# Storing the output projection's rows to DRAM, two more weight buffers, and a new order of the last loads

## The chip, the cores and the metric

The kernel runs on one core of a Trainium2 chip. The metric is the device time of one execution in microseconds. Before the change it is 557.77 us, the median of three runs (557.16 to 558.68).

The engines are named as in the profile: PE is TensorE's matmul and PEld its weight load, DVE is VectorE, ACT is ScalarE, POOL is GpSimd, SP is SyncE, which here only issues transfers. Each has its own queue of instructions, worked off in order.

## The reference

One layer of a decoder trunk on 512 rows of 1024 float32 numbers. Its first part (three kinds of mixers sharing one input and one output projection) ends in `h = h + mix @ w_out`. Then follow the two parts that the change touches:

```python
h = h + hier_moe(rmsnorm(h, norm2_g), router_group_w, ..., exp_w_gate, exp_w_up, exp_w_down)
gate = sigmoid(rmsnorm(h, ple_norm_g) @ ple_gate_w + ple_gate_b)
e = p @ ple_proj_w
h = h + gate * e
return rmsnorm(h, final_norm_g)
```

`hier_moe` picks for every row one group of experts and two experts in it, of 32 in all. Each expert is a gated MLP with two 1024x256 matrices (gate, up) and one 256x1024 matrix (down): 3 MB of weights each, 96 MB together.

## The kernel before, in words

The 512 rows are four tiles of 128 (NT = 4). `h1` holds the rows after the output projection, one tile of 128x1024 each, and stays in SBUF to the end.

**Experts.** They are worked in 16 pairs. A pair gathers up to 64 rows for each of its two experts, from a copy of the normed rows in DRAM (`tnd`), turns them (`xt`), and computes `gu` (gate and up, 16 products), `hid` and `dn` (down, 16 products). The result goes back by an indirect DMA to a table `yd` in DRAM that has two rows for each row of the input. The first pair takes its rows from `h1` by products with a 0/1 matrix (`spread`, L974). The last pair's result is not sent through DRAM: it is added to h1 by products with a 0/1 matrix (`scatter`, L1051), after its rounding error has been split off so that two fast products give full precision.

**Weights.** An expert's weights are three units of 1 MB. A unit takes a buffer from the front of a list, `ring`; a buffer returns to it when the products that read it are recorded, and the transfer itself waits until they have run. `load_units` records loads as long as the ring has buffers. A load also waits until the third load before it has landed (AHEAD = 3). All these transfers, and those of the last stage, are issued by SP in the order in which they are written; that order is fixed by hand, as is PE's order, and ACT's and DVE's from pair 14 on.

**The last stage.** After pair 14, SP loads what the end needs: `load_y(t)`, the two returned rows per input row for tile t (1 MB); the four quarters of the gate matrix (`gate_load`, 1 MB each); and two vectors copied to all partitions (`rows`, 0.5 MB each). The gate product is done in three fast products per block, so the matrix is split: `gate_hi(k, hf)` on ACT scales and rounds block k of column half hf, `gate_lo` on DVE takes the remainder (L1075). For a tile, `add_y` adds the returned rows to h1 (two adds of 128x1024), `scatter` adds the last pair's rows, `turn` transposes the sum and splits it (L1221 to L1224), `rms` takes its mean square (with a power on POOL, L63), `last` runs 48 products per tile (`pg`, L1242), and `finish` does the rest on DVE and ACT (L1252 to L1262) and stores the output. `at` in `tail` puts other work between the products: `prep(t + 1)` turns the next tile, `sums(t)` adds the rows of a later one. Between the last pair's products and the first gate product PE runs 24 products of `pe` (p @ ple_proj_w), which are otherwise spread over the pairs by the table PLE.

Of the kernel before, what the change touches and what calls it, by code (L numbers as in the profile page):

```python
# [27 lines left out]

FILL = (8, 3, 0, 1, 0, 1, 0, 1, 0, 1, 1, 1, 4, 2, 2, 2, 9)

PLE = (5, 1, 1, 1, 1, 1, 1, 1, 1, 1, 1, 1, 1, 1, 2)
PLE_LAST = (4, 4, 4)
AHEAD = 3
NR, NL = 4, 9
CLEAR = (7, 8, 9, 10)
# [53 lines left out]
def mixers(ctx, tc, A, K, dbg):  # L89
# [360 lines left out]
    sbctx.close()  # L450
    pctx.close()
    hp = ctx.enter_context(tc.tile_pool(name="hp", bufs=1, side="left"))
    h1 = K["h1"] = [hp.tile([P, D], F32, name=f"h1_{t}") for t in range(NT)]
    for t in range(NT):
        nc.sync.dma_start(h1[t], A["x"][t * P:(t + 1) * P, :])
    parts = (step for t in range(NT) for hf in range(2) for step in out_proj(nc, K, mixh, mixl, hf, t, WO_EARLY))
# [157 lines left out]
def ffn(ctx, tc, A, K, mixh, mixl, out, dbg, stage):  # L614
# [67 lines left out]

    slab, loads = {}, []

    def load_units(m=96):

        while ring and m and len(slab) < 96:
            n, m = len(slab), m - 1
            n = n - n % 6 + (0, 3, 1, 4, 2, 5)[n % 6]
            slab[n] = unit(F32, [P, 2048])  # L690
            loads.append(nc.sync.dma_start(slab[n], A["w_exp"][n // 3, n % 3]).ins)
            if len(loads) > AHEAD:
                tc.add_manual_dep(loads[-1], loads[-1 - AHEAD].name,
                                  mybir.DependencyInfo(mybir.DependencyClass.Sync, mybir.DependencyReason.DATA))
# [20 lines left out]
    def ple_steps():  # L715

        pT, pW = pl_in
        for j in range(8):
            t, hf = j // 2, j % 2
            p = ps("pe", "sc" if j < 5 else "gu")  # L720
            for c in range(2):
                for k in range(2):
                    n = hf * 512 + c * 256
                    PE.matmul(p[:, c * 256:c * 256 + 256], pT[:, k * S + t * P:k * S + (t + 1) * P], pW[:, k, n:n + 256],  # L724
                              start=(k == 0), stop=(k == 1))
                    if c == k == 1:
                        kept.append((t, hf, p))
                        ple_out()
                    yield
# [14 lines left out]
    V.tensor_copy(cm.rearrange("p a b -> p (a b)"), cmf)  # L744
    V.tensor_tensor(rw, rw, g2c[:, :, None].to_broadcast([P, KC, 36]), ALU.mult)
    tnd = dram.tile([S, D], F32, name="tnd")
    Ab = mw.tile([P, NT, 32], BF, name="Ab")
    pr_ = cw.tile([P, 448], F32, name="pr", tag="cmf")
    posA = pr_[:, :128].rearrange("p (t e) -> p t e", t=NT)
# [87 lines left out]
    def weights(t, g8, e8, id2, c0):  # L837
# [21 lines left out]
        V.tensor_tensor(pe(c0), pe(cw), rt(0), ALU.subtract)  # L859
        V.tensor_copy(rt(1), pe(c0))  # L860
        V.tensor_tensor(rt(2), pe(c0), rt(1), ALU.subtract)

    chosen = {}
    halves = [(t, hf) for t in range(NT) for hf in range(2)]
# [181 lines left out]
    def scatter(j):  # L1046

        t, hf = j // 2, j % 2
        sc = ps("sc", "sc")
        for q in range(2):  # L1050
            PE.matmul(sc, DTs[15][:, t], out_[15][hf][q], start=(q == 0), stop=(q == 1))  # L1051
        y = h1[t][:, 512 * hf:512 * hf + 512]
        V.tensor_tensor(y, y, sc, ALU.add)


    gr, gw = [], {}
# [20 lines left out]
            free(gr[2 * hf + k // 4])  # L1077

    order.enter_context(tc.manual_schedule(engines={mybir.EngineType.PE}))
    load_units(1)  # L1080
    with tc.manual_schedule(engines={mybir.EngineType.DVE}):
        run(steps[0])
        for t in (0, 1):
# [15 lines left out]
        for hf in range(2):  # L1099
            gather_T(0, hf)  # L1100
        one_hot(1, NT - 1)
    ple_load()
    load_units()

# [56 lines left out]
    def add_y(t, rs=(0, 1)):  # L1161

        for r in rs:
            V.tensor_tensor(h1[t], h1[t], ys[t][:, r], ALU.add)  # L1164

    def load_y(t):
        ys.append(unit(F32, [P, 2, D]))
        nc.sync.dma_start(ys[t], yd.rearrange("(r n) d -> n r d", r=2)[t * P:(t + 1) * P])

    ends = ExitStack()  # L1170
    for i in range(16):
# [16 lines left out]
        free(slab[6 * i + 2], slab[6 * i + 5])  # L1188
        load_units()
        if i == 14:  # L1190
            load_y(0)
            for j in range(4):
                gate_load(j)
            load_y(1)
            rows = mix.tile([P, 2, D], F32, name="rows", tag="m0")
            nc.sync.dma_start(rows[:, 0], bcast(A["ple_gate_b"]))
            load_y(2)
            nc.sync.dma_start(rows[:, 1], bcast(A["final_norm_g"]))
            load_y(3)


# [72 lines left out]
    def tail(sums=None):  # L1274

        for t in range(NT):
            at = {}
            if t + 1 < NT:
                at[1, 1] = lambda: prep(t + 1)
            if sums and t == 0:  # L1280
                at[0, 6] = lambda: sums(1)
            if sums and t + 2 < NT:
                at[1, 5] = lambda: sums(t + 2)
            last(t, at)

    def sums(t):
        add_y(t)
        for hf in range(2):
            scatter(2 * t + hf)

    down(15, lambda n: n < 2 and add_y(0, (n,)))
    ple(PLE_LAST[0])
    gate_hi(0, 0)
    for hf in range(2):
        scatter(hf)
    gate_lo(0, 0)
    gate_hi(1, 0)
    ple(PLE_LAST[1])
    lo = [turn(0, hf) for hf in range(2)]
    ple(PLE_LAST[2])  # L1300
    free(pl_in[1])
    for f in lo:
        f()
    gate_lo(1, 0)
    for k in range(2, KC):
        gate_hi(k, 0)
        gate_lo(k, 0)
    count_beyond()
    for k in range(KC):
        gate_hi(k, 1)  # L1310
        gate_lo(k, 1)
    ov_slots = ring[:3]
    junk, h3s = (unit(F32, shape, slot) for shape, slot in zip(([P, 2, 512], [P, 4, 512]), ring[3:]))
    SC.preload_act_table_set("sigmoid_and_others")
    rms(0)
    tail(sums)
    ends.close()
# [157 lines left out]
```

## Time and profile before

| | us |
|---|---|
| median of 3 runs | 557.77 |
| the profiled execution | 556.99 |
| its span | 555.2 |
| PE busy | 514.5 (93% of the span) |
| DVE busy | 276.2 (50%) |
| ACT busy | 210.8 (38%) |
| POOL busy | 87.1 (16%) |
| DMA moved | 148.82 MB, 268 GB/s over the span |

The share of busy time is a mean over stages with different limits. In the timeline a row gives the start, the busy time, the engine, the line, the operation, output and inputs, and in square brackets the idle time of the engine just before it with what ended that. In the chain of waits a row gives start, duration and what the end of the program waited for there. SPq stands for SP's queue of transfers.

### The profile page before, as it was taken

How to read it: one execution, taken by the hardware profiler on the slowest of the kernel's cores; microseconds unless marked ns; L12 is line 12 of the kernel's file. 1: busy time of each engine (PE TensorE's matmuls, PEld its weight loads, DVE VectorE, ACT ScalarE, POOL GpSimd, SP SyncE). 2: the span in 40 equal slices, each digit the busy share in tenths (PEclk: the TensorE clock that was granted, in tenths of full speed). 3: DMA queues.
4: the chain of work that ended last, by engine and by line, in shares of the span. 5: the costliest groups of instructions: out<-in, count | busy, mean ns of one | idle time of the engine just before them, and what ended most of it. 6: DMA issues, size and time to landing. Idle time of an engine off the chain costs nothing.

```text
span 555.2 us, 7581 instructions
## 1 busy us (share of the span) xinstructions
PE 514.5 (93%) x2713; PEld 325.3 (59%) x2713; DVE 276.2 (50%) x735; ACT 210.8 (38%) x443; POOL 87.1 (16%) x122
## 2 busy tenths in 40 slices
PE   8899999999999999999999999998798987949992
PEld 5797886876997788844333333332233332638872
DVE  6762957756747565773422322221121111597764
ACT  7466665646766434411112111110111101473352
POOL 3301111221008500002111111111110000011110
PEclk9999999999999999999999999999999999988997
DMA  8882222300339669989999999999999999950111
GB/s 303 265 325 73 62 72 71 91 26 2 117 126 418 251 263 413 348 337 387 416 412 417 399 394 387 375 383 396 368 399 418 416 418 390 416 211 0 40 44 73
DMA packets 35641, 148.82 MB, mean 268 GB/s; under 512 B 6557, under 2 KB 14109, under 8 KB 22160
## 3 DMA queue, kind: packets, MB, share of 16 engines
q1 hardware_dynamic: 29984, 137.46, 64.3%
q0 software_dynamic: 4320, 7.95, 3.8%
q10 hardware_dynamic: 1296, 2.89, 1.3%
q8 instruction: 23, 0.38, 0.3%
q14 instruction: 18, 0.15, 0.1%
HBM read 139.61 MB, written 16.25 MB: 281 GB/s over the span
## 4 chain that ended last, share of the span: by engine, by line
PE 62%; DMA 18%; DVE 9%; ACT 7%; issue 2%; POOL 1%; SPq 0%; ACTq 0%; DVEq 0%; POOLq 0%
DMA unit<-in_w_exp_dram 17%; PE gu L997 12%; PE pj L234 9%; PE po L80 8%; PE dn L1029 7%; PE pj L257 5%; PE z L257 4%; PE z L311 2%; PE po L333 2%; PE pe L724 2%; ACT unit L1071 2%; PE x L974 1%; DVE h L1164 1%; PE pl L780 1%; PE z L292 1%
## 5 line engine op out<-in xcount | busy, mean ns | idle before, releaser
L997 PE MATMUL gu<-unit,xT 128*64 128x512 f32 x512 | 127.5, 598 | 13.1 <-DMA unit<-in_w_exp_dram 13.1
L997 PEld LDWEIGHTS gu<-unit,xT 128*64 128x64 f32 x512 | 37.0, 137 | 85.0 <-issue 59.2
L1029 PE MATMUL dn<-unit,hidT 128*64 128x512 f32 x256 | 60.6, 599 | 1.7 <-ACT hidT L1020 0.8
L234 PE MATMUL pj<-xh,wp 128*128 128x512 f32 x176 | 51.2, 398 | 0.4 <-ACT wp L69 0.4
L1242 PE MATMUL pg<-unit 128*128 128x512 f32 (+1 forms) x216 | 47.9, 378 | 0.8 <-ACT unit L735 0.6
L1002 ACT ACTIVATE sg<-gu 128x256 f32<-128x256 f32 x16 | 6.1, 383 | 110.5 <-PE gu L997 110.5
L1003 DVE SCALAR_TENSOR_TENSOR hid<-sg,wsl,gu 128x256 f32<-128x256 f32 x16 | 7.7, 478 | 79.6 <-ACT sg L1002 79.5
L1242 PEld LDWEIGHTS pg<-unit 128*128 128x128 f32 x216 | 37.9, 193 | 9.0 <-ACT unit L735 0.7
L1043 POOL DMA_INDIRECT yd<-big,idy x15 | 15.1, 1009 | 163.8 <-ACT big L1033 163.8
L1029 PEld LDWEIGHTS dn<-unit,hidT 128*64 128x64 f32 x256 | 19.7, 137 | 32.0 <-issue 24.2
L234 PEld LDWEIGHTS pj<-xh,wp 128*128 128x128 f32 x176 | 32.6, 188 | 8.2 <-ACT wp L69 1.3
L1033 ACT ACTIVATE big<-dn 128x512 f32<-128x512 f32 x30 | 17.9, 597 | 50.0 <-PE dn L1029 50.0
L930 DVE COPY SL<-sl 128x10 f32<-128x10 f32 (+1 forms) x17 | 2.8, 167 | 66.0 <-PE sl L929 66.0
L70 DVE TENSOR_TENSOR wp<-wraw,wp 128x768 fp32r<-128x768 f32 (+2 forms) x28 | 25.8, 927 | 13.6 <-ACT wp L69 13.4
L69 ACT ACTIVATE wp<-wraw 128x768 fp32r<-128x768 f32 (+2 forms) x28 | 22.8, 817 | 20.2 <-PE pj L234 9.8
L234 PE MATMUL pj<-xl,wp 128*128 128x512 f32 x88 | 29.4, 401 | 0.0
L986 DVE TENSOR_TENSOR xT<-xt,g2c 128x512 f32<-128x512 f32 x30 | 20.6, 687 | 11.8 <-PE xt L985 11.7
L80 PE MATMUL po<-wo,mx 128*128 128x512 f32 x96 | 25.7, 408 | 0.0
L257 PE MATMUL pj<-wp,xh 128*128 128x384 f32 x96 | 24.8, 351 | 0.0
L80 PE MATMUL po<-unit,mx 128*128 128x512 f32 x96 | 24.1, 399 | 0.0
L943 POOL DMA_INDIRECT xg<-tnd,idx x15 | 15.4, 1029 | 33.7 <-issue 16.0
L985 PEld LDWEIGHTS xt<-ident,xg 128*128 128x128 f32 x120 | 13.4, 141 | 11.5 <-issue 11.4
(293 smaller groups left out, 881.2 us busy)
## 6 DMA issues: line engine op xcount, KB each, us to landing
unit<-in_w_exp_dram SPq DMA_DIRECT2D x96, 1024.0 KB, 8.7
wraw<-in_w_in_dram SPq DMA_DIRECT2D x20, 384.0 KB, 3.5
yd<-zero SPq DMA_DIRECT2D x4, 1024.0 KB, 7.9
unit<-yd SPq DMA_DIRECT2D x4, 1024.0 KB, 6.5
unit<-in_ple_gate_w_dram SPq DMA_DIRECT2D x4, 1024.0 KB
wraw<-in_w_out_dram SPq DMA_DIRECT2D x8, 256.0 KB, 3.0
h<-in_x_dram SPq DMA_DIRECT2D x4, 512.0 KB
unit<-in_w_out_dram SPq DMA_DIRECT2D x4, 512.0 KB, 7.8
```

The source lines that it names most:

```text
L69: nc.scalar.activation(h, src, AF.Copy)
L70: nc.vector.tensor_tensor(l, src, h.bitcast(F32), ALU.subtract)
L80: nc.tensor.matmul(p, a[k][:, ts_], K["wo"][k][:, b, hs], start=(n == 0), stop=(n == 3 * len(ks) - 1))
L234: PE.matmul(q, a[:, i * P:(i + 1) * P], b[k], start=(n == 0), stop=(n == 3 * KC - 1))
L257: PE.matmul(p[t][:, :W_IN[j]], a[k][:, t * P:(t + 1) * P], b, start=(n == 0), stop=(n == 3 * KC - 1))
L943: G.indirect_dma_start(out=xg[i % 2], out_offset=None, in_=tnd, in_offset=bass.IndirectOffsetOnAxis(ap=idx[:, i:i + 1], axis=0), bounds_ch ...
L986: V.tensor_tensor(xTs[i, hf], p.rearrange("p (a b) -> p a b", a=4), g2c[:, 4 * hf:4 * hf + 4, None].to_broadcast([P, 4, P]), ALU.mult)
L997: PE.matmul(gu[64 * e:64 * e + 64], xTs[i, k // 4][:, k % 4, 64 * e:64 * e + 64], w[e][k // 4][:, 512 * (k % 4):512 * (k % 4) + 512], star ...
L1029: PE.matmul(dn[64 * e:64 * e + 64], hT[:, f, 64 * e:64 * e + 64], w[e][2][:, 1024 * f + 512 * hf:1024 * f + 512 * hf + 512], start=(f == 0 ...
L1033: SC.activation(o[:, 512 * hf:512 * hf + 512], dn, AF.Copy)
L1043: G.indirect_dma_start(out=yd, out_offset=bass.IndirectOffsetOnAxis(ap=idy[:, i:i + 1], axis=0), in_=o, in_offset=None, bounds_check=2 * S ...
L1242: PE.matmul(p, hT[t][:, a, ks], gw[k][:, b, hs], start=start and n == 0, stop=stop and n == len(ab) - 1)
```

## The change

h1 becomes two buffers of two tiles each. As soon as all four tiles are complete they are stored to a DRAM tensor `hd`, and when the first pair has read them, the two buffers join the ring as two more units. Two more weight loads are recorded ahead of these stores. Near the end h1 is loaded back: tile 0 ahead of the last two weight units, the others between the returned rows. The first gate quarter is loaded ahead of tile 0's returned rows and partly split inside the last pair's down step. The adds of the returned rows move from DVE to POOL for tiles 1 to 3. The last pair's rows are added to tile 1 behind the weight splits, by products recorded earlier. More `pe` products go into the pairs, so that 4 are left for the end.

```diff
-PLE = (5, 1, 1, 1, 1, 1, 1, 1, 1, 1, 1, 1, 1, 1, 2)
-PLE_LAST = (4, 4, 4)
+PLE = (5, 1, 1, 1, 1, 1, 2, 2, 2, 2, 2, 2, 2, 2, 2)
+PLE_LAST = 4
...
-    h1 = K["h1"] = [hp.tile([P, D], F32, name=f"h1_{t}") for t in range(NT)]
+    K["hp"] = hp
+    hh = [hp.tile([P, 2, D], F32, name=f"h1_{j}", tag=f"h{j}") for j in range(2)]
+    h1 = K["h1"] = [hh[t // 2][:, t % 2] for t in range(NT)]
...
+    def load_h(t):
+
+        if t % 2 == 0:
+            back.append(unit(F32, [P, 2, D]))
+        h1[t] = back[-1][:, t % 2]
+        nc.sync.dma_start(h1[t], hd[t * P:(t + 1) * P, :])
...
         while ring and m and len(slab) < 96:
+            if len(slab) == 94 and not back:
+                load_h(0)
+                continue
...
-            p = ps("pe", "sc" if j < 5 else "gu")
+            p = ps("pe", "sc" if j < 7 else "gu")
...
+    def store_h(t):
+        nc.sync.dma_start(hd[t * P:(t + 1) * P, :], h1[t])
...
-        V.tensor_tensor(y, y, sc, ALU.add)
+        return lambda: V.tensor_tensor(y, y, sc, ALU.add)
...
-    load_units(1)
+    load_units(3)
+    for t in range(NT):
+        store_h(t)
...
+    ring.extend(((K["hp"], "h0"), (K["hp"], "h1")))
     ple_load()
     load_units()
...
-            V.tensor_tensor(h1[t], h1[t], ys[t][:, r], ALU.add)
+            (G if t else V).tensor_tensor(h1[t], h1[t], ys[t][:, r], ALU.add)
...
         if i == 14:
+            gate_load(0)
             load_y(0)
-            for j in range(4):
-                gate_load(j)
+            gate_load(1)
+            load_h(1)
             load_y(1)
+            gate_load(2)
+            gate_load(3)
...
-                at[1, 1] = lambda: prep(t + 1)
-            if sums and t == 0:
-                at[0, 6] = lambda: sums(1)
+                at[1, 1 if t else 6] = lambda: prep(t + 1)
             if sums and t + 2 < NT:
+                at[0, 0] = lambda: add_y(t + 2)
                 at[1, 5] = lambda: sums(t + 2)
...
+    def behind_down(n):
+        if n == 0:
+            SC.preload_act_table_set("sigmoid_and_others")
+            for k in range(4):
+                gate_hi(k, 0)
+            for k in range(3):
+                gate_lo(k, 0)
+        if n < 2:
+            add_y(0, (n,))
+
+    down(15, behind_down)
+    ple(PLE_LAST)
+    for f in [scatter(hf) for hf in range(2)]:
+        f()
+    gate_lo(3, 0)
     lo = [turn(0, hf) for hf in range(2)]
-    ple(PLE_LAST[2])
     free(pl_in[1])
+    add_y(1)
     for f in lo:
         f()
-    gate_lo(1, 0)
-    for k in range(2, KC):
+    second = [scatter(2 + hf) for hf in range(2)]
+    for k in range(4, KC):
         gate_hi(k, 0)
         gate_lo(k, 0)
-    count_beyond()
     for k in range(KC):
         gate_hi(k, 1)
         gate_lo(k, 1)
+    for f in second:
+        f()
+    count_beyond()
```

What the change moves shows in the order of the instructions in two places. The first is SP's queue from the last weights on, before the change and then with it (`unit` is a buffer of the ring, the tensor behind the arrow says what is loaded).

```order
L691 DMA unit<-in_w_exp_dram 128x2048 x80
L1168 DMA unit<-yd 128x2x1024
L1060 DMA unit<-in_ple_gate_w_dram 128x2048 x4
L1168 DMA unit<-yd 128x2x1024
L1196 DMA rows<-in_ple_gate_b_dram 128x1024
```

```order
L705 DMA unit<-in_w_exp_dram 128x2048 x76
L692 DMA unit<-hd 128x1024
L705 DMA unit<-in_w_exp_dram 128x2048 x2
L1078 DMA unit<-in_ple_gate_w_dram 128x2048
L1189 DMA unit<-yd 128x2x1024
L1078 DMA unit<-in_ple_gate_w_dram 128x2048
L692 DMA unit<-hd 128x1024
L1189 DMA unit<-yd 128x2x1024
L1078 DMA unit<-in_ple_gate_w_dram 128x2048 x2
L1220 DMA rows<-in_ple_gate_b_dram 128x1024
L692 DMA unit<-hd 128x1024
```

Between the last weights and the first returned rows (`yd`) there stood nothing, and now a gate quarter; tile 0 of h1 (`hd`) stands ahead of the last two weight units.

The second is DVE's queue. Before the change it is shown from tile 0's scatter adds on, ahead of which stood only the adds of tile 0's returned rows and the splits of the down product; with the change from the last pair's `hid` on. L1164/L1185 are the adds of the returned rows, L1057 the splits of the down product, L1075/L1093 gate_lo, L1053/L1071 the scatter's adds, L1224/L1250 the turned rows.

```order
L1053 TENSOR_TENSOR h_0_1508<-h_0_1508,sc 128x512 x2
L1075 SCALAR_TENSOR_TENSOR unit<-unit,g3c 128x512
L1224 TENSOR_TENSOR unit<-xt,unit 128x512 x2
L1075 SCALAR_TENSOR_TENSOR unit<-unit,g3c 128x512 x7
L1136 CAST on<-pov 1x1
L1075 SCALAR_TENSOR_TENSOR unit<-unit,g3c 128x512 x8
L1208 TENSOR_SCALAR ms<-pm 128x1
L1210 SCALAR_TENSOR_TENSOR ms<-pm,ms 128x1
L1164 TENSOR_TENSOR h_1_1509<-h_1_1509,unit 128x1024 x2
L1053 TENSOR_TENSOR h_1_1509<-h_1_1509,sc 128x512 x2
```

```order
L1093 SCALAR_TENSOR_TENSOR unit<-unit,g3c 128x512 x3
L1185 TENSOR_TENSOR unit<-unit 128x1024
L1057 TENSOR_TENSOR unit<-dn,unit 128x512
L1185 TENSOR_TENSOR unit<-unit 128x1024
L1057 TENSOR_TENSOR unit<-dn,unit 128x512
L1071 TENSOR_TENSOR unit<-unit,sc 128x512 x2
L1093 SCALAR_TENSOR_TENSOR unit<-unit,g3c 128x512
L1250 TENSOR_TENSOR unit<-xt,unit 128x512 x2
L1093 SCALAR_TENSOR_TENSOR unit<-unit,g3c 128x512 x12
L1071 TENSOR_TENSOR unit<-unit,sc 128x512 x2
L1157 CAST on<-pov 1x1
L1234 TENSOR_SCALAR ms<-pm 128x1
```

Three gate_lo now stand ahead of tile 0's adds, and tile 1's two adds are gone from DVE. They stand on POOL, whose queue behind the last indirect DMA is now as follows (`rsp` and `rsl` are the powers of `rms` and `finish`; before, only these stood there).

```order
L1185 TENSOR_TENSOR unit<-unit 128x1024 x2
L63 TENSOR_TENSOR rsp<-ms,mhalf 128x1
L1185 TENSOR_TENSOR unit<-unit 128x1024 x3
L63 TENSOR_TENSOR rsp<-ms,mhalf 128x1
L1185 TENSOR_TENSOR unit<-unit 128x1024
L63 TENSOR_TENSOR rsl<-ms,mhalf 128x1
```

The adds of tile 2 and the first of tile 3 stand behind tile 0's power, and tile 3's second add behind tile 1's.

## Rows read from the trace of the kernel before

**Rows 1.** The page, its 40 equal slices of the span: busy share of PE and of the 16 DMA engines in tenths.

```profile
PE   8899999999999999999999999998798987949992
...
DMA  8882222300339669989999999999999999950111
```

**Rows 2.** Whom SP's queue waited for: line, releaser, us in total, times, longest.

```profile
SPq L691 <- DMA unit<-in_w_exp_dram: 221.6, 84, 8.7
...
SPq L691 <- PE gu L997: 8.0, 5, 4.2
SPq L691 <- PE po L80: 7.6, 4, 4.5
```

**Rows 3.** The chain of waits where the experts end.

```profile
457.86 9.15 DMA unit<-in_w_exp_dram
...
467.05 1.93 PE gu L997 x6
...
473.15 3.65 PE dn L1029 x16
```

**Rows 4.** The timeline: tile 0's returned rows, issued and waited for.

```profile
468.27 0.38 SPq L1168 DMA_DIRECT2D unit<-yd  x1
...
474.75 1.23 DVE L1164 TENSOR_TENSOR h<-h,unit 128x1024 f32<-128x1024 f32 x1 [2.57 <-DMA unit<-yd]
```

**Rows 5.** The timeline: a split of the down product on DVE, the gate matrix's splits on ACT and on DVE.

```profile
475.89 0.68 DVE L1039 TENSOR_TENSOR unit<-dn,unit 128x512 fp32r<-128x512 f32 x1
...
484.52 8.68 ACT L1071 ACTIVATE unit<-unit,g3c 128x512 fp32r<-128x512 f32 x14
...
489.32 5.37 DVE L1075 SCALAR_TENSOR_TENSOR unit<-unit,g3c 128x512 fp32r<-128x512 f32 x8
```

**Rows 6.** The timeline: tile 1's scatter adds, and PE's wait for them.

```profile
498.54 1.29 DVE L1053 TENSOR_TENSOR h<-h,sc 128x512 f32<-128x512 f32 x2
499.29 1.57 PEld L1221 LDWEIGHTS xt<-ident,h 128*128 128x128 f32 x8 [7.62 <-DVE h L1053]
499.29 1.97 PE L1221 MATMUL xt<-ident,h 128*128 128x128 f32 x8 [7.18 <-DVE h L1053]
```

**Rows 7.** Busy time by stretch: length, then PE, PEld, DVE, ACT and POOL with instructions, then the granted clock of PE as a share of full speed (0.50 and 1.00 are 1.2 and 2.4 GHz), the DMA share and GB/s.

```profile
496.50:497.00 0.50, 0.00 (x0) 0.00 (x0) 0.50 (x1) 0.00 (x0) 0.50 (x1) 0.73 0.00 0
...
499.00:503.50 4.50, 4.21 (x14) 3.73 (x15) 3.56 (x6) 1.37 (x4) 0.00 (x0) 0.50 0.00 0
503.50:504.00 0.50, 0.50 (x3) 0.38 (x3) 0.15 (x1) 0.50 (x2) 0.00 (x0) 0.94 0.00 0
```

**Rows 8.** The page, DMA queues: packets, MB, their time as a share of 16 engines' span.

```profile
q10 hardware_dynamic: 1296, 2.89, 1.3%
```

**Rows 9.** Busy time by stretch around the end of the output projection, columns as in rows 7; the last two are the DMA share and GB/s.

```profile
226.00:230.00 4.00, 4.00 (x24) 3.31 (x23) 2.61 (x15) 0.57 (x2) 0.00 (x0) 1.00 0.78 258
230.00:244.00 14.00, 12.80 (x107) 10.70 (x107) 9.89 (x51) 3.13 (x7) 0.54 (x1) 1.00 1.00 380
244.00:248.00 4.00, 4.00 (x21) 1.18 (x18) 3.44 (x19) 1.84 (x7) 1.24 (x1) 1.00 0.55 184
...
252.00:254.00 2.00, 1.96 (x16) 1.59 (x16) 0.89 (x3) 0.38 (x1) 0.99 (x1) 1.00 0.89 324
254.00:262.00 8.00, 8.00 (x42) 2.61 (x40) 1.74 (x9) 1.20 (x2) 2.05 (x2) 1.00 1.00 390
```

**Rows 10.** First POOL's tensor_tensor of 128x1024 as a group (busy us, mean ns of one, idle before), then from the timeline other tensor_tensor of POOL beside DVE's operations.

```profile
L677 POOL TENSOR_TENSOR unit<-unit 128x1024 fp32r<-128x1024 f32 x2 | 4.7, 2372 | 0.0
...
14.53 0.74 DVE L179 SCALAR_TENSOR_TENSOR xl<-xr,g,xh 128x512 fp32r<-128x512 f32 x1
...
16.13 2.04 POOL L183 TENSOR_TENSOR gs<-gs,xr 128x512 f32<-128x512 f32 x1 [2.07 <-ACT xr L181]
16.94 1.78 DVE L179 SCALAR_TENSOR_TENSOR xl<-xr,g,xh 128x512 fp32r<-128x512 f32 x1
...
168.12 1.85 POOL L382 TENSOR_TENSOR gs<-gs,gng 128x384 f32<-128x384 f32 x1 [17.43 <-DVE sig L367]
...
170.05 1.01 POOL L383 TENSOR_TENSOR gs<-gs,sig 128x384 f32<-128x384 f32 x1
```

**Rows 11.** The timeline: `finish` of tile 0, its first operation, the sigmoid and the product with e, and a later power on POOL.

```profile
499.75 0.74 DVE L1252 SCALAR_TENSOR_TENSOR unit<-pg,rsp,rows 128x512 f32<-128x512 f32 x1
500.58 0.63 ACT L1253 ACTIVATE unit<-unit 128x512 f32<-128x512 f32 x1 [4.73 <-DVE unit L1252]
501.25 0.69 DVE L1254 TENSOR_TENSOR unit<-unit 128x512 f32<-128x512 f32 x1 [0.76 <-ACT unit L1253]
...
513.51 0.54 POOL L63 TENSOR_TENSOR rsl<-ms,mhalf 128x1 f32<-128x1 f32 x1 [6.10 <-DVE ms L1210]
```

**Rows 12.** The timeline: PE's scatter products, gate products and transposes, and DVE's first operation on the products of tiles 1, 2 and 3 (for tile 3 its last piece).

```profile
504.98 1.09 PE L1051 MATMUL sc<-unit,xT 128*128 128x512 f32 x4
...
505.91 8.50 PE L1242 MATMUL pg<-unit 128*128 128x512 f32 x36
...
514.25 1.03 PE L1221 MATMUL xt<-ident,h 128*128 128x128 f32 x8
514.56 0.74 DVE L1252 SCALAR_TENSOR_TENSOR unit<-pg,rsp,rows 128x512 f32<-128x512 f32 x1
...
529.25 0.74 DVE L1252 SCALAR_TENSOR_TENSOR unit<-pg,rsp,rows 128x512 f32<-128x512 f32 x1
...
546.38 0.48 DVE L1252 SCALAR_TENSOR_TENSOR unit<-pg,rsp,rows 128x256 f32<-128x256 f32 x1
```

More of the change, by code (lines that the diff above doesn't have):

```diff
@@ L683, in ffn @@
     slab, loads = {}, []
+    def load_h(t):
[3 more added lines that the diff above has]
+        nc.sync.dma_start(h1[t], hd[t * P:(t + 1) * P, :])
+    back = []
     def load_units(m=96):
         while ring and m and len(slab) < 96:
+            if len(slab) == 94 and not back:
+                load_h(0)
+                continue
             n, m = len(slab), m - 1
@@ L746, in ffn @@
     tnd = dram.tile([S, D], F32, name="tnd")
+    hd = dram.tile([S, D], F32, name="hd")
     Ab = mw.tile([P, NT, 32], BF, name="Ab")
@@ L1190, in ffn @@
         if i == 14:
+            gate_load(0)
             load_y(0)
-            for j in range(4):
-                gate_load(j)
+            gate_load(1)
+            load_h(1)
             load_y(1)
+            gate_load(2)
+            gate_load(3)
             rows = mix.tile([P, 2, D], F32, name="rows", tag="m0")
             nc.sync.dma_start(rows[:, 0], bcast(A["ple_gate_b"]))
+            load_h(2)
             load_y(2)
             nc.sync.dma_start(rows[:, 1], bcast(A["final_norm_g"]))
+            load_h(3)
             load_y(3)
@@ L1286, in sums @@
     def sums(t):
-        add_y(t)
         for hf in range(2):
[L1289 to L1298, printed above, removed]
+            scatter(2 * t + hf)()
+    def behind_down(n):
[12 more added lines that the diff above has]
+    gate_lo(3, 0)
     lo = [turn(0, hf) for hf in range(2)]
-    ple(PLE_LAST[2])
     free(pl_in[1])
+    add_y(1)
     for f in lo:
         f()
-    gate_lo(1, 0)
-    for k in range(2, KC):
+    second = [scatter(2 + hf) for hf in range(2)]
+    for k in range(4, KC):
         gate_hi(k, 0)
         gate_lo(k, 0)
-    count_beyond()
     for k in range(KC):
@@ L1311, in ffn @@
         gate_lo(k, 1)
+    for f in second:
+        f()
+    count_beyond()
     ov_slots = ring[:3]
     junk, h3s = (unit(F32, shape, slot) for shape, slot in zip(([P, 2, 512], [P, 4, 512]), ring[3:]))
-    SC.preload_act_table_set("sigmoid_and_others")
     rms(0)
```

## The prediction

> **What bounds the kernel now.** I read the page's row of slices first: TensorE is busy all along except near the end, and the DMA row stands at 9 from just before the middle to seven eighths of the span [rows 1]. So one stretch is bound by transfers and the end by something else. The list of who the SP queue waited for says what holds the transfers back: in 84 places the next expert-weight load waits for an earlier one to land, 221.6 us in all, and for a buffer that TensorE has to release it waits for 8.0 and 7.6 us [rows 2]. A load may be issued only when the third before it has landed, so this is a full DMA queue and not a lack of buffers. The chain of waits then gives the place where this stage ends: a weight transfer lands at 467.01, then come the last gate/up products, the activation and at 473.15 the last down product [rows 3]. Behind it the end has its own limits, of which the reader is to see four: the returned rows of the first tile (y0 below) land at 474.75 and the add waits for them [rows 4]; ScalarE and VectorE then split the gate weights back to back until about 494.7 [rows 5]; TensorE sits idle 7.18 us before 499.29, until VectorE has added the second tile's rows, at 498.54 [rows 6]; and the clock it is granted falls to 0.50 in that wait and is back only at 503.5 [rows 7].
>
> The sum is made against the profiled execution: 556.99 us, of which 555.2 are span; the median of the runs shown is 557.77, so 0.8 is added at the end.
>
> **The stores (slower by 2.4).** Four stores move 2.1 MB of h1 to DRAM. Of stores the trace has the ACT queue (q10, which stores tnd and the output): 2.89 MB took 1.3% of the span, 7.2 us [rows 8], so 2.1 MB are 5.2 us of all 16 engines. What they displace are weights, since 84 of the 96 loads wait for another load [rows 2]. They cost nothing only where the DMA was idle, and where two more buffers let it work. At full rate it moves about 416 GB/s. In 244 to 248 it moved 184, so (416-184) x 4 = 928 KB are free, 2.2 us: here the ring was empty until the first expert's weights were released, and here the two units help. 252 to 254 gives 0.4. 226 to 230 ran at 258, 1.5 us free, but the first extra load waits for a buffer of w_out that the last output products release only in that stretch, and its bytes follow its issue later still, so I take 0.2 of it [rows 9]. 5.2 - 2.8 = 2.4: the last gate/up weights land at 469.4. Bounds: if every shortfall from 226 to 262 is filled (1.5 + 1.2 + 2.2 + 0.4 + 0.5 = 5.8) it is -0.6; if nothing is filled, +5.2. The extra buffers by themselves bring nothing else, as a stream that is full to the end ends when its bytes are through, however early each was issued. The other additions here are hidden: 8 more ple products of 0.4 us lie in a stage in which TensorE waits for weights.
>
> **The order of the last transfers (slower by 3.9).** Transfers of one queue come in one after another: from 467.01 to 474.75 three of 1 MB land (two down weights and y0), 2.58 us each. The new order puts half a megabyte (h1 of tile 0) ahead of the two down weights and a gate quarter ahead of y0: 1.5 x 2.58 = 3.9. y0 lands at 474.75 + 2.4 + 3.9 = 481.0, the gate quarter at 478.5. ScalarE now splits four blocks of it (8.68/14 = 0.62 each, [rows 5]) before it copies the down product, whose first half is ready near 477.4 (its start at 475.6 plus half of 3.65, [rows 3]); but VectorE would wait for y0 anyway, so this delay is covered, and the three blocks that VectorE splits there are done when y0 comes. The down product starts up to 0.4 later than its operand, as its second weight lands about 475.9; that too lies before y0. Bounds of the step: 0 if y0's landing were not awaited (its own wait of 2.57 us in [rows 4] excludes it) and 5.2 with a whole transfer for the half.
>
> **From y0 to the end.** VectorE's order is fixed, so I add its rows. Two adds of y0 at 1.23 [rows 4] and two splits of the down product at 0.68 [rows 5]: 484.8. The two scatter adds (1.29 as in [rows 6], and 0.3 for TensorE's last scatter product): 486.4. One weight split and the two residuals of the turned rows, which read PSUM as the scatter adds do: 0.74 + 1.29, so 488.4. Twelve weight splits at 5.37/8 = 0.67: 496.4 if alone.
>
> They are not alone. The adds of tiles 1 to 3 move to GpSimd. There a 128x1024 add of two SBUF operands takes 2372 ns [rows 10], against 1.23 on VectorE. And the two get in each other's way: a VectorE split of 128x512 takes 0.74 at 14.53, but 1.78 at 16.94, where it stands still until GpSimd's tensor_tensor of 16.13 is through [rows 10]. The Trainium skill states this as a rule ("SBUF — State Buffer", Who interferes with whom): a VectorE instruction with two SBUF inputs contends with a GpSimd instruction that reads SBUF, whichever starts first keeps the shared ports for the whole instruction, and the other is blocked. By that rule, and [rows 10] agree with it, the end comes out as summed below; without it, as in rival (a).
>
> So tile 1's two adds, which begin when y1 lands (y0 + 2.5 transfers = 487.5), hold up the weight splits by 2 x 2.37, less 0.9 beside the turned rows: 3.8. Splits end at 500.2, tile 1's scatter adds at 501.5 (before: 499.83). Then 0.8 for the mean and the power (0.54 of it on GpSimd), 0.74 for the first operation on tile 0's product, 0.63 for its sigmoid: 503.8 with the hand-overs [rows 11]. Here three VectorE operations with two SBUF inputs meet three GpSimd adds that stand ready (two of tile 2, one of tile 3, all queued behind that power): they alternate. GpSimd until 504.7, 0.7, GpSimd until 507.8, 0.7, GpSimd until 510.9, 0.7 and 0.1: 511.7. Scatter adds of tile 2, 1.29, then the first residual of tile 1's turned rows, 0.68: 513.7. Of VectorE's waits for GpSimd this counts 3.8 before 502 and 5.7 behind it; the bounds are 0, if the two don't meet, and six adds of 2.37, 14.2, if none lay beside anything; I stay with the count, since the row at 16.94 shows a wait to the end of the other's instruction. TensorE has run out of other work by then: since the turn of tile 1 now stands after all but two steps of tile 0, the only thing that it has after about 505 is tile 1, whose third product waits for this residual.
>
> From there TensorE paces the rest: 142 products of tiles 1 to 3 at 8.50/36 = 0.236 (33.5), 0.5 for the last half in two pieces, 16 transposes (2.1) and 4 scatter products (1.1): 37.2 [rows 12]. The wait of 8 us has two products in it, so whether the clock falls as in [rows 7], where 4.5 us at 0.50 cost 2.2, is open; I take half, 1.1. Products end at 552.0. Then 0.3 to VectorE's last piece, and from its start to the end of the span 8.8, as before (546.38 to 555.2) [rows 12]: 561.1. That is 5.9 over 555.2. Before, tile 2's first VectorE operation came 14.69 after tile 1's and TensorE alone would need 13.4 (48 products, 8 transposes, 4 scatter products); that slack is what the moved adds do give back, and it is in the 37.2.
>
> 557.77 + 5.9 gives 563.7 us.
>
> **Rivals.** (a) GpSimd's adds run beside VectorE and cost it nothing. Then splits end at 496.4, tile 1's adds at 497.7, the first finish at 502.1; tile 2's scatter adds wait for GpSimd until 503.2 and the residual is there at 505.2, when TensorE has just come to it, so its clock stays up: 505.2 + 37.2 + 9.1 = 551.5, 3.7 faster, 554.1 us. The point from which this decides is VectorE's wait behind 502.3: under 1 us in all, it is this case. For it: GpSimd's spans are rough in the profile, and the rows show the block on few instructions. Against it: both directions of the block stand in the trace with the same shapes. (b) VectorE keeps its ports through back-to-back operations and GpSimd gets in only behind them, and the idle DMA is filled entirely: the second GpSimd add comes after the splits, the third after the finish. That takes off 2.4, the stores 3.0, the clock 1.1: 557.2, no change. For it: at 168.12 a GpSimd tensor_tensor of 128x384 took 1.85, where the next one took 1.01 [rows 10]. Against it: the split of 16.94 did stand still. (c) The change does not do what it says: the two units fill no idle time, because loads queue behind stores that wait for h1. The stores' term is then 5.2 and not 2.4: 566.5 us. Against it: the stall of 244 to 248 is one of empty buffers.
>
> **How the numbers follow.** Chances: forecast 0.45, (a) 0.30, (b) 0.13, (c) 0.12. A measurement of this kernel can tell 0.3%, 1.7 us, from no change. Faster is (a) and a small share of (b): 0.32. Same is most of (b): 0.13. Slower is the forecast and (c): 0.55. The range reaches from 553.0, into the middle of (a), to 567.5, over (c); within the forecast alone (the stores from -0.6 to +5.2 about 2.4, the clock 1.1 each way) it is 559.6 to 567.6.
>
> **What would show it.** Right: the last gate/up weight lands near 469.4, y0 near 481; weight splits beside GpSimd's adds last over 1.5 us, as do the products with eo, h1 and the final gain in tile 0; TensorE waits about 8 us before tile 1's third product. Wrong: the weights end at or before 467, which would say that buffers and not bytes held the stream; or splits stay at 0.74 beside a GpSimd add, and then (a) is what happened.

## The result, and the profile after it

The changed kernel takes 560.81 us (median of 13 runs, 558.06 to 563.57) against 557.16 us for the kernel before on the same chip (13 runs): 1.0071 times, 95% interval 1.0047 to 1.0095, so 2.6 to 5.3 us slower. The profiled execution took 561.99 us with a span of 560.1, 4.9 more than the 555.2 of before. I had forecast 563.7, 5.9 slower, mainly by three terms: stores, the order of the last transfers, and GpSimd's adds in VectorE's way.

Not all of the 4.9 need be work of the change. This is busy time by stretch near the start of the program, far ahead of everything that was changed, before and after (columns as in [rows 7]):

```profile
20.00:22.00 2.00, 0.63 (x3) 0.19 (x1) 0.83 (x2) 1.09 (x2) 1.36 (x1) 1.00 0.54 50
22.00:24.00 2.00, 1.86 (x12) 1.74 (x13) 1.96 (x4) 0.00 (x0) 0.00 (x0) 1.00 0.88 328
24.00:26.00 2.00, 2.00 (x11) 1.74 (x11) 0.93 (x1) 0.87 (x1) 1.04 (x1) 1.00 0.95 393
```

```profile
20.00:22.00 2.00, 0.70 (x5) 0.27 (x3) 0.96 (x2) 0.96 (x2) 1.00 (x1) 1.00 0.56 56
22.00:24.00 2.00, 2.00 (x11) 1.81 (x11) 1.61 (x3) 0.28 (x1) 0.31 (x1) 0.64 0.99 390
24.00:26.00 2.00, 2.00 (x7) 1.52 (x6) 0.99 (x1) 0.59 (x1) 0.73 (x1) 0.50 0.97 381
```

Behind a short wait (1.50 us before, 1.30 after) TensorE's granted clock stayed at 1.00 in the one execution and fell to 0.50 in the other. The sixth of the eight groups of transposes of the router's input starts at 225.25 before and at 226.51 after: up to there 1.26 us are lost. Eight of the fourteen profiled executions have this fall, with and without every part of the change, so it is no work of the change. How much of it reaches the end is not shown. The profiled execution of one run below (h1 kept, adds on VectorE, gate quarter behind the rows) comes to these transposes at 229.51, 4.26 later than the kernel before, and its last gate/up products start only 0.65 later (467.70 against 467.05). The difference to explain is therefore that of the medians, 3.65; a figure of the profile may hold up to 1.26 that the change did not cause.

Now the page's slices and SP's waits of the changed kernel, against [rows 1] and [rows 2]:

```profile
PE   8999999999999999988999999999899887885993
...
DMA  9782222310439669999999999999999999970111
```

```profile
SPq L705 <- DMA unit<-in_w_exp_dram: 224.5, 87, 9.4
...
SPq L705 <- DMA hd<-h: 10.0, 3, 6.8
SPq L705 <- PE po L80: 9.7, 6, 4.6
```

The 8 in the DMA row before the middle has become a 9, and TensorE's row has a 7 and a 5 near its end, where it had two 7s and a 4: by this row alone the end looks no worse. The loads now also wait 10.0 us for the stores to leave h1's buffers. By stretch, against [rows 9]:

```profile
226.00:230.00 4.00, 4.00 (x30) 3.64 (x30) 2.63 (x13) 1.21 (x3) 0.00 (x0) 1.00 0.82 270
230.00:244.00 14.00, 12.79 (x110) 11.19 (x110) 9.80 (x47) 2.84 (x5) 0.54 (x1) 1.00 1.01 384
244.00:248.00 4.00, 4.00 (x21) 1.42 (x22) 3.50 (x24) 2.14 (x7) 0.00 (x0) 1.00 1.05 436
...
252.00:254.00 2.00, 2.00 (x10) 1.47 (x8) 1.41 (x9) 0.00 (x0) 0.03 (x1) 1.00 0.98 410
254.00:262.00 8.00, 5.21 (x23) 2.23 (x24) 1.35 (x2) 0.61 (x2) 0.96 (x1) 0.79 1.03 421
```

The stall of 244 to 248 is filled: 436 GB/s, where 184 were. From the experts' end on, the timeline has (in the order of [rows 3, 4, 5, 6, 11, 12]):

```profile
469.06 1.37 PE L1015 MATMUL gu<-unit,xT 128*64 128x512 f32 x4 [2.08 <-DMA unit<-in_w_exp_dram]
...
478.80 2.08 DVE L1093 SCALAR_TENSOR_TENSOR unit<-unit,g3c 128x512 fp32r<-128x512 f32 x3 [3.02 <-DMA unit<-yd]
480.57 0.38 SPq L1189 DMA_DIRECT2D unit<-yd  x1
480.80 1.22 DVE L1185 TENSOR_TENSOR unit<-unit 128x1024 f32<-128x1024 f32 x1
...
487.11 5.20 POOL L1185 TENSOR_TENSOR unit<-unit 128x1024 f32<-128x1024 f32 x2 [22.96 <-DMA unit<-yd]
487.62 11.88 DVE L1093 SCALAR_TENSOR_TENSOR unit<-unit,g3c 128x512 fp32r<-128x512 f32 x12
...
499.41 1.27 DVE L1071 TENSOR_TENSOR unit<-unit,sc 128x512 f32<-128x512 f32 x2
...
501.71 7.89 POOL L1185 TENSOR_TENSOR unit<-unit 128x1024 f32<-128x1024 f32 x3
501.76 0.75 DVE L1278 SCALAR_TENSOR_TENSOR unit<-pg,rsp,rows 128x512 f32<-128x512 f32 x1 [0.68 <-POOL rsp L63]
...
503.27 1.38 DVE L1280 TENSOR_TENSOR unit<-unit 128x512 f32<-128x512 f32 x1 [0.76 <-ACT unit L1279]
504.68 2.71 DVE L1281 TENSOR_TENSOR unit<-unit 128x512 f32<-128x512 f32 x1
507.43 2.73 DVE L1283 TENSOR_TENSOR unit<-unit,rows 128x512 f32<-128x512 f32 x1
...
512.07 3.35 PE L1268 MATMUL pg<-unit 128*128 128x512 f32 x7 [2.10 <-DVE unit L1250]
...
551.11 0.48 DVE L1278 SCALAR_TENSOR_TENSOR unit<-pg,rsp,rows 128x256 f32<-128x256 f32 x1
```

The reader is to see both places at which VectorE stands still beside a GpSimd add: the twelve splits in 11.88 (0.67 each would be 8.0; the first two, beside the two adds, take 2.44 and 2.89), and three operations with 1.38, 2.71 and 2.73 where 0.69 is usual. An operation with an operand in PSUM (501.76, `pg`) takes its usual 0.75 beside the same add. The bracket of 478.80 names y0's transfer, but SP's load of 480.57 waited for y0's landing, so y0 was there only then; what the split needs first is the block that ScalarE begins at 478.05. TensorE restarts at 512.07, on a clock that has fallen:

```profile
507.00:512.00 5.00, 1.22 (x2) 0.50 (x2) 4.96 (x7) 2.91 (x8) 2.61 (x1) 0.53 0.00 0
512.00:517.30 5.30, 5.23 (x12) 4.13 (x13) 4.42 (x8) 0.64 (x2) 2.89 (x2) 0.50 0.00 0
```

### The profile page after: what moved, and what is told of

It is laid out like the page before. It is cut to its first block, busy times and chain, and to the rows that moved or that the text cites. A ratio compares the mean times of both kernels' runs of the same rounds, so it can differ in the third digit from the quotient of the medians.

```text
span 560.1 us, 7609 instructions
## 1 busy us (share of the span) xinstructions
PE 517.6 (92%) x2713; PEld 325.5 (58%) x2713; DVE 280.2 (50%) x729; ACT 210.9 (38%) x443; POOL 99.7 (18%) x128
## 3 DMA queue, kind: packets, MB, share of 16 engines
q10 hardware_dynamic: 1296, 2.89, 1.3%
## 4 chain that ended last, share of the span: by engine, by line
PE 69%; DMA 17%; DVE 5%; issue 3%; ACT 2%; POOL 1%; SPq 1%; POOLq 0%; ACTq 0%; DVEq 0%
PE gu L1015 13%; DMA unit<-in_w_exp_dram 10%; PE pj L234 9%; PE dn L1047 8%; PE po L80 8%; PE pg L1268 5%; PE pj L257 5%; PE z L257 4%; DMA unit<-yd 2%; PE z L311 2%; PE po L333 2%; DMA yd<-big,idy 1%; DMA xg<-tnd,idx 1%; PE xt L1003 1%; PE x L992 1%
## 5 line engine op out<-in xcount | busy, mean ns | idle before, releaser
L1268 PE MATMUL pg<-unit 128*128 128x512 f32 (+1 forms) x216 | 49.8, 388 | 7.5 <-ACT unit L1249 4.3
L1003 PE MATMUL xt<-ident,xg 128*128 128x128 f32 x120 | 18.8, 279 | 2.8 <-DMA xg<-tnd,idx 2.8
```

The lines of the kernel that those rows point to most:

```text
L1003: PE.transpose(p[:, k * P:(k + 1) * P], xg[i % 2][:, (4 * hf + k) * P:(4 * hf + k + 1) * P], ident)
L1268: PE.matmul(p, hT[t][:, a, ks], gw[k][:, b, hs], start=start and n == 0, stop=stop and n == len(ab) - 1)
```

## The experiments

Every ratio is to the kernel before, run on the same chip; medians of before were 556.4 to 556.9 us. Where a run is put so many us from another, that is the difference of their ratios times 557. My theory: GpSimd's adds block VectorE, and the traffic of h1 delays the experts' end. Rivals: the adds are harmless and the traffic does it all; or one wait hides the other.

### Taking the adds back, keeping h1, and both

Adds of tiles 1 to 3 on VectorE, behind the splits and ahead of the scatter adds:

```diff
-            (G if t else V).tensor_tensor(h1[t], h1[t], ys[t][:, r], ALU.add)
+            V.tensor_tensor(h1[t], h1[t], ys[t][:, r], ALU.add)
...
-    add_y(1)
...
+    add_y(1)
     for f in second:
...
-                at[0, 0] = lambda: add_y(t + 2)
...
     def sums(t):
+        add_y(t)
```

> The changed kernel with the adds of tiles 1 to 3 back on VectorE: tile 1's behind the last weight split, those of tiles 2 and 3 directly before their scatter adds, as in the kernel before. Transfers stay as changed. Theory of the blocked VectorE: the twelve weight splits from 487.6 take about 8.3 us and not 11.88, the four operations of tile 0's first finish follow each other without waits for GpSimd, the third product of tile 1 starts near 509.2 and not at 512.1, the last output is issued about 3.2 us earlier than 554.35; time 557.6, ratio to before 1.000. Rival, GpSimd's adds relieve VectorE and only the transfers make the changed kernel slower: six adds of 1.23 come back to VectorE's order, 561 to 564.5 us, ratio 1.007 to 1.013.

Measured: 558.0 us, ratio 1.0022 (0.9997 to 1.0046), 2.7 us below the changed kernel.

```profile
488.26 8.04 DVE L1093 SCALAR_TENSOR_TENSOR unit<-unit,g3c 128x512 fp32r<-128x512 f32 x12
...
496.23 2.47 DVE L1185 TENSOR_TENSOR unit<-unit 128x1024 f32<-128x1024 f32 x2
...
502.68 0.69 DVE L1280 TENSOR_TENSOR unit<-unit 128x512 f32<-128x512 f32 x1 [0.76 <-ACT unit L1279]
503.41 0.69 DVE L1281 TENSOR_TENSOR unit<-unit 128x512 f32<-128x512 f32 x1
504.13 0.69 DVE L1283 TENSOR_TENSOR unit<-unit,rows 128x512 f32<-128x512 f32 x1
...
509.56 5.68 PE L1268 MATMUL pg<-unit 128*128 128x512 f32 x13 [3.37 <-DVE unit L1250]
```

Splits and finish are back at their own durations, and the third product of tile 1 starts 21.3 us after the splits' begin, not 24.45. So the adds hold VectorE up by more than they relieve it of, and the rival (harmless adds) falls.

h1 kept in SBUF:

```diff
-    load_units(3)
-    for t in range(NT):
-        store_h(t)
+    load_units(1)
...
-    ring.extend(((K["hp"], "h0"), (K["hp"], "h1")))
```

(and without the reloads).

> The changed kernel with h1 kept in SBUF: no stores, no reloads, no two extra weight buffers; the order of the other transfers, the adds on GpSimd and the order of the engines as changed. Theory that transfers cost: the last gate/up weights land at 467.0 (469.06 in the changed kernel), the rows of tile 0 are there by 477.3 and not 480.5, the third product of tile 1 starts near 508.5, the end moves by 3.3 to 3.9; time 557.2, ratio 0.999 to 1.001. Rival, the waits for GpSimd's adds set the end and take the gain back: third product within 1 us of 512.1, time 560 to 561.

Measured: 559.2 us, ratio 1.0046 (1.0025 to 1.0067): 1.4 us below the changed kernel, against 3.3 to 3.9 expected. Its third product started at 509.41 in the profile, near the theory's 508.5, but the timed gain is nearer to the rival's. Both edits together:

> Both of the first two edits: h1 kept in SBUF (no stores, no reloads, no extra buffers) and all adds on VectorE. What is left of the change is the gate quarter ahead of tile 0's rows, the turn of tile 1 behind all but two steps of tile 0, and the other spread of the ple products. If the two costs stand one behind the other they add up to 6.5: third product of tile 1 near 505, time 554.3, ratio 0.994. Rival, they are two names of one wait: 557, ratio 1.000.

Measured: 555.31 us, ratio 0.9976 (0.9958 to 0.9994), between the 0.994 of the theory and the 1.000 of the rival. That is faster than before. The single steps from the changed kernel won 2.7 and 1.4, together 4.1, both at once win 5.3, so within the intervals the two costs add up: from here h1's way through DRAM adds 0.0046 (2.6 us, to the first run of this section) and GpSimd's adds another 0.0049 (2.7 us, to the changed kernel). The other path gives 3.9 for the adds and 1.4 for h1; intervals of 0.2% each way cover the difference.

The two places of the wait were parted by moving tile 1's adds alone:

```diff
-            (G if t else V).tensor_tensor(h1[t], h1[t], ys[t][:, r], ALU.add)
+            (G if t > 1 else V).tensor_tensor(h1[t], h1[t], ys[t][:, r], ALU.add)
```

> The changed kernel with tile 1's two adds on VectorE, behind the last weight split; those of tiles 2 and 3 stay on GpSimd. It parts the two places at which I count a wait. Theory of the blocked VectorE: the twelve splits take 8.0 to 8.3 us in place of 11.88, of which tile 1's adds take 2.5 back; in tile 0's first finish the operations with eo, h1 and the final gain still take turns with three adds (2.7 us for the second and third of them in place of 0.69); third product of tile 1 0.5 to 1.5 us earlier against the splits' start, time 1 us below the changed kernel, ratio 1.005. Rival, only the first place costs and the second lies beside other waits: as with all adds on VectorE, ratio 1.002.

Measured: 560.8 us, ratio 1.0085 (1.0048 to 1.0122), which tells nothing apart. Its trace does: splits 8.04, the three operations of the finish as slow as in the changed kernel, third product 23.68 after the splits' begin. So of the 3.15 us between 24.45 and 21.3, 0.8 belong to the first place and 2.4 to the second.

And the adds alone, put into the kernel before (the same line, nothing else):

> The kernel before with the adds of tiles 1 to 3 on GpSimd and nothing else changed. Theory of the blocked VectorE: the adds of tile 1 (near 488) and of tile 2 stand beside weight splits and hold them up by about 2.4 us each, splits end 3.5 to 5 us later than before, tile 0's first finish takes turns with the rest; VectorE is rid of 6 adds of 1.23, so what is left is 1 to 2.5 us slower, ratio 1.002 to 1.0045. Rival, the two run beside each other: VectorE gains 3.7 us, ratio 0.993 to 0.995.

Measured: 558.96 us, ratio 1.0051 (1.0027 to 1.0075), 2.8 us slower.

```profile
484.89 7.68 DVE L1075 SCALAR_TENSOR_TENSOR unit<-unit,g3c 128x512 fp32r<-128x512 f32 x5
486.36 11.18 POOL L1164 TENSOR_TENSOR h<-h,unit 128x1024 f32<-128x1024 f32 x4 [25.02 <-DMA unit<-yd]
...
492.56 8.18 DVE L1075 SCALAR_TENSOR_TENSOR unit<-unit,g3c 128x512 fp32r<-128x512 f32 x6
...
505.97 2.76 DVE L1255 TENSOR_TENSOR unit<-unit,h 128x512 f32<-128x512 f32 x1
```

Four adds beside eleven splits, which take 15.9 us in place of 7.4. Here the adds are the only difference.

### The place of the gate quarter

```diff
-            gate_load(0)
             load_y(0)
+            gate_load(0)
```

(with its splits behind the scatter adds again.)

> The changed kernel with the first gate quarter behind tile 0's rows again, and the seven splits of it (four on ScalarE, three on VectorE) behind the scatter adds, as before; all else as changed. The rows of tile 0 land 2.6 us earlier, at 477.9. My sum of the steps says that the four splits of VectorE that now come behind the rows take as much as is won: 4 x 0.67 = 2.7, so that the third product of tile 1 starts between 512 and 514.7 and the time is 561 to 562.2, ratio 1.007 to 1.010. Rival, the place of tile 0's rows in the queue is what delays the end: everything 2.6 earlier, 558.2, ratio 1.002.

Measured: 559.86 us, ratio 1.0072 (1.0044 to 1.0099), the changed kernel's own. The same exchange without h1's traffic and with all adds on VectorE:

> Like the run with h1 kept in SBUF and all adds on VectorE, but with the first gate quarter behind tile 0's rows again and its splits behind the scatter adds, as in the kernel before. What is left of the change is the turn of tile 1 behind all but two steps of tile 0, tile 1's adds directly behind the splits, and the spread of the ple products. If the gate quarter's place is worth nothing, as the splits moved ahead of the rows take what the rows lose: 555.3 us, ratio 0.9976 as with the quarter ahead. If the quarter ahead is what makes that run faster than the kernel before: 556.7, ratio 1.000. If the rows' place in the queue decides: 553, ratio 0.993.

Measured: 554.16 us, ratio 0.9956 (0.9933 to 0.9979), against 0.9976 with the quarter ahead. Twice the quarter's place makes no difference that can be measured: the rows come 2.6 us later, and four splits of 0.67 are out of the way by then. What this kernel still has of the change is chiefly the turn of tile 1, the places of tile 1's rows and adds and the ple spread, and it is faster than before; which of these does it was not tried.

### Stores and buffers apart

> The changed kernel without its four stores: the reloads read the input x in place of the stored h1, so the output lacks the mixers' part; two extra weight buffers, reloads and everything else as changed. Theory of my sum (bytes: 2.1 MB stored are 5.2 us of transfers, and idle transfer time is filled by weights instead): the last gate/up weights land 4 to 5 us earlier than in the changed kernel, counted from the transposes near 226, and the time falls by as much, 556 us, ratio 0.998 to 1.000. Rival, the stores lie in transfer time that was idle anyway: the weights land less than 1.5 us earlier and the time is within 1.5 us of the changed kernel, ratio 1.0045 to 1.007.

Measured: 554.51 us, ratio 0.9965 (0.9936 to 0.9994), 5.9 us below the changed kernel.

```profile
230.00:244.00 14.00, 12.80 (x108) 10.89 (x108) 9.88 (x48) 2.84 (x5) 0.54 (x1) 1.00 1.00 406
244.00:248.00 4.00, 4.00 (x22) 1.29 (x18) 3.50 (x23) 2.14 (x7) 1.24 (x1) 1.00 1.01 424
```

```profile
460.57 1.93 PE L1014 MATMUL gu<-unit,xT 128*64 128x512 f32 x6 [1.70 <-DMA unit<-in_w_exp_dram]
```

The products that wait for the last gate/up weights start at 460.57. That is 8.5 before the changed kernel's 469.06, of which 0.8 is there already at the transposes (225.71 against 226.51); I had expected 4 to 5. In time the stores cost 5.9, which agrees with the 5.2 of their bytes within the intervals, so the rival falls. But the weights also come 6.5 us before those of the kernel before (467.05), and 5.4 before those of the run that keeps h1 and differs from this one in the buffers, the two loads recorded earlier and the reloads alone (465.93). The two buffers bring that, where I had given them 2.8.

The stores alone, in the kernel before:

```diff
     load_units(1)
+    for t in range(NT):
+        nc.sync.dma_start(hd[t * P:(t + 1) * P, :], h1[t])
```

> The kernel before with the four stores of h1 alone: the rows are stored at the place where the changed kernel stores them and never read again; no extra buffers, no reloads, nothing moved. Theory of my sum: without the two buffers the idle transfer time from 244 to 248 stays empty, so at most 0.2 to 0.6 us of the 5.2 are hidden; the last gate/up weights land 4.6 to 5 us later than before, counted from the transposes near 225, time 561.5, ratio 1.008 to 1.009. Rival, stores share the engines with weight loads so that more is hidden: weights 1 to 2 us later, ratio 1.002 to 1.004.

Measured: 558.81 us, ratio 1.0049 (1.0023 to 1.0076), 2.7 us slower, not 4.5 to 5.

```profile
244.00:248.00 4.00, 4.00 (x24) 1.56 (x24) 3.33 (x23) 2.14 (x7) 0.00 (x0) 1.00 1.01 424
...
254.00:262.00 8.00, 5.72 (x31) 2.41 (x30) 1.35 (x2) 1.49 (x3) 0.99 (x1) 1.00 1.02 418
```

```profile
470.13 1.08 PE L998 MATMUL gu<-unit,xT 128*64 128x512 f32 x4 [1.08 <-DMA unit<-in_w_exp_dram]
```

The idle stretch of 244 to 248 is filled here without any extra buffer: the stores have put the weight loads back, and those catch up in it. (SP issues no load between 236.41 and 248.67, so what moves there was issued ahead of the stall.) The rival was nearer: the last weights are 3.1 later, and the same transposes were already 1.7 late; this execution has the clock's fall near 22 us too.

Stores and buffers thus fill the same idle time. The last gate/up products start at 466.9 with neither (mean of five executions), at 470.1 with the stores alone (one), at 462.0 with the buffers alone (four: this section's first and the three of the next), and at 468.5 with both (four). So the buffers bring 4.9 without the stores and 1.7 with them, and the stores cost 3.2 without the buffers and 6.5 with them.

### A version from what was learned

The buffers are worth having, the stores are not. The normed rows `tnd`, which lie in DRAM for the experts anyway, are h1 times a factor r per row. So h1 can be reloaded from them, and the first add of the returned rows multiplies by 1/r in the same instruction:

```diff
-        nc.sync.dma_start(h1[t], hd[t * P:(t + 1) * P, :])
+        nc.sync.dma_start(h1[t], tnd[t * P:(t + 1) * P, :])
...
-            (G if t else V).tensor_tensor(h1[t], h1[t], ys[t][:, r], ALU.add)
+            if r == 0:
+                V.scalar_tensor_tensor(h1[t], h1[t], rt_inv[t], ys[t][:, r], ALU.mult, ALU.add)
+            else:
+                V.tensor_tensor(h1[t], h1[t], ys[t][:, r], ALU.add)
```

> A version built on what the other runs showed: no stores of h1 at all, since the normed rows tnd, which lie in DRAM anyway, are h1 times a factor per row; the reloads read tnd, and the first add of each tile multiplies by the factor's reciprocal in the same instruction. The two extra buffers stay, all adds are on VectorE, the rest is as changed. If the costs add up (no store: 5.9 below the changed kernel; adds on VectorE: 2.7 below it), 552 us, ratio 0.990 to 0.994; the last gate/up weights land near 461 as without the stores. Rival, the multiplying add is slower than the plain one of 1.22, or the end of VectorE's chain takes the gain: 555 to 556 us, ratio 0.996 to 0.999.

Measured: 553.6 us, ratio 0.9941 (0.9918 to 0.9965), at the upper edge of what the theory gave; the last gate/up products start at 462.26. With tile 0's rows ahead of the gate quarter again:

> The version that reloads h1 from the normed rows, with the first gate quarter behind tile 0's rows again and its splits behind the scatter adds, as in the kernel before. By the sum of VectorE's chain the quarter's place is worth nothing here either: 553.6 us, ratio 0.994. If the small gain of the earlier pair of runs (0.9976 with the quarter ahead, 0.9956 behind) is real, 552.5, ratio 0.992.

Measured: 553.94 us, ratio 0.9948 (0.9924 to 0.9972): a third time no difference. Last, the adds of tiles 2 and 3 where the changed kernel issues them, on VectorE:

> The same with the adds of tiles 2 and 3 ahead of the finish of the tile two before, where the changed kernel issues them, but on VectorE: their 2.5 us stand before the first product is waited for and in the time in which VectorE waits for the sigmoid. Theory: 0.7 us less than with the adds directly before the scatter adds, ratio 0.991 to 0.993; rival, the order makes tile 0's finish late and the end with it: no gain, ratio 0.994 to 0.996.

Measured: 550.13 us, ratio 0.9884 (0.9842 to 0.9926), 3.6 us below the run before it and not 0.7 (the intervals allow 0.9 to 6.2).

```profile
499.26 1.29 DVE L1182 SCALAR_TENSOR_TENSOR unit<-unit,ri 128x1024 f32<-128x1024 f32 x1
...
503.85 7.62 PE L1267 MATMUL pg<-unit 128*128 128x512 f32 x25 [3.44 <-DVE unit L1249]
```

```profile
493.58 1.28 DVE L1182 SCALAR_TENSOR_TENSOR unit<-unit,ri 128x1024 f32<-128x1024 f32 x1
...
501.81 6.07 PE L1267 MATMUL pg<-unit 128*128 128x512 f32 x25 [0.77 <-DVE unit L1249]
```

The first fence is the run before, the second this one. There tile 2's adds stand behind tile 0's finish, right ahead of the scatter adds and of the residual for which TensorE's third product of tile 1 waits; here they stand ahead of that finish. TensorE waits 0.60 and 0.77 in place of 3.44, and its next 25 products take 6.07 in place of 7.62: the granted clock is 1.00 from 501.8 to 509, where the other run has 0.65 from 503.8 to 507 and 0.87 from there to 511.5. From these products on TensorE runs to the end without another such wait in both, so they set the end. VectorE's last piece comes 3.5 earlier in this profile (539.32 against 542.85). Of that, 1.1 is there already when the weight splits end (489.32 against 490.40), ahead of everything that was moved; 1.0 is the earlier third product, near the 0.7 that I had counted, and 1.5 is the clock, which I had left out. The multiplying add takes 1.28, little more than the plain one. This version beats both kernels.

## Why the prediction was right, and where it was off

The forecast's mechanism happened and its rivals did not, but the term of the stores came out near by luck. Step by step:

- **The stores** (2.4, last weights at 469.4). The changed kernel's landed at 469.06. Four executions with the changed transfers end this stage at 466.93, 468.59, 469.06 and 469.31, five with h1 in SBUF and no stores at 465.93, 466.01, 467.05, 467.70 and 467.78: on average 1.6 apart, with two executions in each group that have the early fall. One of the four lies below the 467 that I had named as a sign of being wrong, so single executions scatter too much for that sign. The stretches of 226 to 262 fit the 1.6: (436-184) x 4 + (410-324) x 2 + (421-390) x 8, and 0.1 MB ahead of them, are 1.5 MB or 3.7 us filled, not 2.8, and 5.2 - 3.7 = 1.5. What failed is the sentence that the extra buffers bring nothing else: without stores they bring 4.9, and the stores alone already fill the stall. The cost of 5.2 came out larger too, 6.5 beside the buffers by the averages above. That the net of two such terms came out nearly right is luck.
- **The order of the last transfers** (3.9). From the last gate/up products' start to the first add of y0: 7.70 before, 11.74 after, so 4.04. The add starts right behind the third split, and y0 was there at 480.57 (predicted 481.0). As the sum had it, the quarter's share of this is returned by the four splits; three pairs of runs show it.
- **VectorE beside GpSimd, first place** (3.8). 11.88 - 8.04 = 3.8. **Second place** (5.7). From the first operation of tile 0's finish to the end of its last: 8.40 in the changed kernel, 3.65 with the adds on VectorE: 4.75. The three waits were 0.7, 2.0 and 2.0, not 0.9, 2.4 and 2.4. The Trainium skill's rule ("SBUF — State Buffer", Who interferes with whom) fits the splits of 2.44 and 2.89 beside the adds, and the unblocked 0.75 with an operand in PSUM too.
- **TensorE's restart** (513.7): 512.07, 1.0 earlier by the second place and 0.6 by an earlier start of tile 0's finish. From its last product of tile 0, at 504.44, to the third of tile 1 are 7.6 us with two products between, as forecast (8).
- **The clock** (1.1, half of a fall): it fell fully. The 5.23 us of work at half speed behind the restart cost 2.6; the two products ahead of it ran at half speed too, but in a wait.
- **From the restart on** (37.2 + 1.1 + 0.3): 39.0 to VectorE's last piece at 551.11, where I had 38.6; without the clock's 2.6 that is 36.4 and not 37.5, so TensorE's work was counted 1.1 too long. The slack that moved adds give back is there: tile 2's first operation comes 12.94 after tile 1's, before 14.69 [rows 12].

Together that is 3.65 by the medians and 4.9 in the profile, against 5.9. In the profile y0's add lies 0.2 ahead of the forecast, the sigmoid of tile 0 0.5, the restart 1.6, the last piece 1.2 and the end 1.0; if the early fall's 1.26 reaches them whole, each lies 1.26 further ahead. The terms that missed most are the second place, by 1.0, the clock, by 1.5, and TensorE's work, by 1.1 the other way; the stores missed by 0.8 as a net, and by more in each of their two halves. Rival (a) is excluded by the two runs that moved the adds alone; (b) by both of tile 1's adds, which are through at 492.31 while the splits run to 499.5, and by the 2.7 at 504.68 and 507.43; (c) by the filled stall, although its fear was justified in part: loads do wait for stores.

## What to carry to other kernels

Before you move VectorE's adds to GpSimd, look what VectorE does at that time: with two operands in SBUF on both sides they take turns by whole instructions, and here six adds of 1.23 saved cost more than they gave. A buffer that is bought with extra traffic should be priced as two terms, what the buffer brings and what the bytes take, with a look at whether both fill the same idle time; then ask whether the data already lies in DRAM in another form. And compare a stretch ahead of the change in both profiles before you read one behind it.

## What had not been expected

- TensorE's granted clock fell to 0.50 (0.60 in one) between 22 and 26 us in eight executions and stayed at 1.00 in six, with the same instructions. The wait ahead does not part them: it is 1.06 to 2.14 us with the fall, and 1.50 to 2.06 without it in four; the other two have no wait.
- The stores' traffic made the first gather late: TensorE waits 2.75 us for it ahead of 256.8 (0.18 in the run without stores), and its clock is 0.79 from 254 to 262. That lies in a stage that waits for weights anyway, and no run shows that it costs time.
- From 226 to 262 the run without stores moved 397 GB/s and the kernel before 349: 1.7 MB, or 4.2 of the 6.5 us that the weights come earlier. Where the rest is won is not shown: from 350 to 400 the four runs with the buffers and no stores moved 379 to 392 GB/s, and the five with neither 377 to 398.
